# Two down projections of layer 0 as seven block products, and layer 1's late weight sums moved behind the second half of attention

## The chip, the core and the metric

The kernel runs on one core of one Trainium2 chip. A core has five engines that each work through a list of instructions of their own, in order, and wait for one another by semaphores: TensorE (PE in the profile; PEld is its loading of weights), VectorE (DVE), ScalarE (ACT), GpSimd (POOL) and SyncE (SP). Work is held in SBUF, 128 partitions wide; matmuls write to PSUM, which has eight banks of 512 float32 per partition. Transfers to and from the chip's memory (HBM) run on 16 DMA engines; here SP issues the loads of weights and POOL issues the transfers that form sums of weights.

The metric is the device time in microseconds (us), median of the runs shown. Lower is better.

## The reference, cut to what matters

A decoder trunk of two layers takes 1024 prompt tokens and 8 sample tokens, with model width 1024 and FFN width 2816 (22 slices of 128). Each layer is a mixer and a SwiGLU FFN, each with a norm before and after it and a residual sum.

```python
def swiglu(h, w_gu, w_down):
    gate, up = jnp.split(h @ w_gu, 2, axis=-1)
    return (jax.nn.silu(gate) * up) @ w_down
...
for l in range(DEPTH):
    g = g_norm[l]
    hn = rmsnorm(h, g[0])
    if l < N_A:
        mix, S = a_mixer(hn, w_in_a[l], lbs[l], hg_norm[l], mem_k[l], mem_v[l], w_o[l], hg_s0[l])
    else:
        mix = b_mixer(hn, w_in_b[l - N_A], sb_bias[l - N_A], k_all, v_all, q_pos, k_pos,
                      mem_k[l], mem_v[l], w_o[l])
    h = h + rmsnorm(mix, g[1])
    h = h + rmsnorm(swiglu(rmsnorm(h, g[2]), w_gu[l], w_down[l]), g[3])
    if l == N_A - 1:
        sb_k, sb_v = jnp.split(rmsnorm(h, g_kv) @ w_kv, 2, axis=-1)
```

`a_mixer` (layer 0) is a gated linear recurrence beside attention into a memory of 256 tokens; `b_mixer` (layer 1) is stick-breaking attention over one shared K and V beside the same kind of memory attention. Both end in a product with `w_o`, the output projection.

## The kernel before, in words

**Tokens and products.** The tokens are cut into two groups: group 0 has 512 of the prompt, group 1 has the other 512 and the 8 samples, 520 columns in all, worked as two halves of 260. Activations lie transposed, 128 features on the partitions and tokens along the columns. Every float32 operand is split into a high part in the matmul type fp32r and the remainder as a second fp32r. One product of 128x128 weights is then three matmuls for each block of columns: high by high, high by low, low by high. A weight tile of 128x512 (256 KB) is loaded by SP, cast by ACT and subtracted by DVE (`split_w`, lines 212, 217 and 218; `split_to`, lines 238 and 239, for other operands). Five raw and five split weight tiles can be under way at once.

**proj.** `proj` (line 231 issues its matmuls) makes one output block of 128 features from K input slices. Its result stands in a tile `mm` of two PSUM banks, one for each half of the columns; there are two such tiles. Beside them PSUM holds three one-bank tiles `s` and one `ns`.

**An FFN.** `ffn` works in five parts of the 22 slices, `PARTS = [(0, 5), (5, 5), (10, 4), (14, 4), (18, 4)]`. In each part it first makes the 4 or 5 gate-up slices (a `proj` for gate, one for up, `silu`, a product on line 1037, and the split of the result), then the down projection of these slices: eight `proj`, one for each 128 of the 1024 outputs, each added by DVE to the residual tile `R` in `evac_raw` (line 553, one addition of 128x520). This is the form that layer 0 uses for both groups, and layer 1 for group 0.

**Block products.** Layer 1's group 1 uses `ffn_w`. There two output blocks by two input slices are multiplied as a 2x2 block matrix with seven block products in place of eight (Strassen's scheme in Winograd's form). In `down_w` (matmul on line 841) a product is 12 matmuls of 260 columns: two output blocks, two input slices, three of the split. For each half of the outputs there are 7 products, accumulated in eight one-bank accumulators, four (`q` = 0 to 3) for each of the two output blocks (`i` = 0, 1). ACT copies an accumulator negated into another one (`minus`, line 854), and DVE adds the accumulators to `R` in pieces of 128x260 (`add`, line 850). The scheme needs four sums of weight blocks, and sums of the gate-up results of two slices.

**Sums of weights.** They are formed in DRAM by transfers that POOL issues: `weight_sums` for the gate-up weights, `down_sums` for the down weights. Each block takes eight steps (`summed`, lines 740 to 754): a one-column copy on ACT (`rr`, line 747, three buffers), a copy of that on POOL (`mk`, line 748), and then a transfer (a copy, line 753, or an accumulation, line 751) that waits for the transfers it reads from. POOL works in order, so a transfer that waits also holds up the steps behind it. What the ACT copy reads is the step's release: before, it is a column of the FFN that runs beside it.

**The order of the work.** The program is written as generators. `weave` takes the next piece of the stream that is furthest behind by its rate; a scheduler places the instructions on the engines from there. The stretch around the change, for group 1 of layer 0:

```python
f1 = ffn(1, 0, o1.x)
ws = weight_sums(1, range(5), lambda: f1.now, 4)
weave((chain(b0.sb(), b0.mem()), 24), (chain(f1.part(0), f1.part(1)), 18), (islice(ws, 16), 17))
weave((chain(f1.part(2), f1.part(3), f1.part(4)), 24), (ws, 24))
```

`b0` is the layer-1 mixer of group 0; `a0`, `a1` are layer 0's mixers of group 0 and 1; `o0.mm` and `o1.mm` are output projections, `o0.finish` and `o1.finish` the norm, the residual and the next norm behind them, `b1.sb` the attention of group 1.

Of the kernel before, what the change touches and what calls it, by code (L numbers as in the profile page):

```python
# [24 lines left out]
def tile_decoder(  # L25
# [180 lines left out]

    def split_w(W, k0, nk, m0):
        out = []
        for a in range(0, nk, 4):
# [8 lines left out]
            nc.vector.tensor_sub(ws[:, 1, :n, :], raw[:, :n, :], ws[:, 0, :n, :].bitcast(F32))  # L218
            for i in range(n):
                out.append((ws[:, 0, i, :], ws[:, 1, i, :]))  # L220
# [412 lines left out]

    def gate_up_w(l, f, ops, spl, raws, pair=None):
# [52 lines left out]
        mt = M(F32R)  # L687

        def put_sum(dst, d, a, b):
            nc.vector.tensor_sub(d, a, b)  # L690
            split_to((dst[:, 0], dst[:, 1]), d)

        if not pair:
            w = n if pair is None else h
            split_to((mt[:, 0, :w], mt[:, 1, :w]), sg[:, :w])
            if pair is not None:
                put_sum(mt[:, :, h:n], sg[:, :h], sg[:, h:n], sg[:, :h])
                pair.append((mt, sg))
            return mt
        m0, s0 = pair.pop()  # L700
        split_to((mt[:, 0, :n], mt[:, 1, :n]), sg[:, :n])
        y = [bpool.tile([P, 2, h], F32R, tag="b", name=nm("ys")) for _ in range(3)]
        put_sum(y[2], s0[:, h:n], s0[:, h:n], sg[:, h:n])
        put_sum(y[1], sg[:, h:n], sg[:, h:n], s0[:, :h])
        put_sum(y[0], sg[:, :h], sg[:, :h], sg[:, h:n])
        pair.extend((m0[:, :, :h], mt[:, :, :h], mt[:, :, h:n], y[0], m0[:, :, h:n], y[1], y[2]))
        return mt
# [26 lines left out]
    def down_sums(l, parts, after):  # L734
        for i in parts:
            t = [tc.dram_tile([P, 2, 512], F32, name=nm("dsum")) for _ in range(4)]
            dsums[i] = t
            yield from summed(t, *down_blocks(l, PARTS[i][0]), after)
# [17 lines left out]
    dsums = {}  # L756
    htok, done = [], []
# [3 lines left out]
    class ffn_w:  # L761
# [47 lines left out]
        def down_w(self, pi, f0, pairs, extra):  # L809
            l, n, h, R = self.l, NG[1], PW[1], self.R  # L810
            a11, a12, a21, a22 = down_blocks(l, f0)
            s1, s2, s3, s4 = dsums[pi]
            src = ((a11, 0), (s1, 4), (s2, 5), (a12, 1), (s3, 6), (s4, 2), (a22, 3))
            for m0 in (0, 2):
                ms = (m0, m0 + 1)
                acc = [[Q(i) for i in range(4)] for _ in ms]

                def weight(rows):
                    r = self.raws().rearrange("p k m -> p (k m)")
                    nc.sync.dma_start(r.rearrange("p (t c) -> p t c", t=2), rows[:, :, m0 * P : (m0 + 2) * P])  # L820
                    w = self.spl()
                    split_to((w[:, 0, :], w[:, 1, :]), r)
                    return w

                def slice_of(q, hf, a, first=False):
                    for i in range(2):
                        o = hf * 256 + i * P
                        for wi, (wj, xi) in enumerate(((0, 0), (0, 1), (1, 0))):
                            nc.tensor.matmul(
                                acc[i][q][:, :h], we[:, wj, o : o + P], extra[0][:, xi, a * h : (a + 1) * h],  # L830
                                start=(first and wi == 0), stop=(wi == 2), skip_group_check=True,
                            )

                def product(q, j, first=False):
                    w = weight(src[j][0])
                    for i in range(2):
                        for t in range(2):
                            x = pairs[t][src[j][1]]
                            o = t * 256 + i * P
                            for wi, (wj, xi) in enumerate(((0, 0), (0, 1), (1, 0))):  # L840
                                nc.tensor.matmul(  # L841
                                    acc[i][q][:, :h], w[:, wj, o : o + P], x[:, xi, :],
                                    start=(first and t == 0 and wi == 0), stop=(t == 1 and wi == 2),
                                    skip_group_check=True,
                                )

                def add(q, mo, a, sub=False):
                    for i, m in enumerate(ms):
                        d = R[m + mo][:, a * h : (a + 1) * h]
                        (nc.vector.tensor_sub if sub else nc.vector.tensor_add)(d, d, acc[i][q][:, :h])  # L850

                def minus(q, p):
                    for i in range(2):
                        nc.scalar.activation(acc[i][q][:, :h], acc[i][p][:, :h], AF.Copy, scale=-1.0)

                product(0, 0, True)
                minus(1, 0)
                product(3, 1, True)
                product(1, 2)
                minus(2, 1)  # L860
                product(0, 3)
# [1146 lines left out]
```

## Time and profile before

| what | value |
|---|---|
| time, median of 3 runs | 2417.74 us (2417.72 to 2418.53) |
| the profiled execution's own time | 2418.81 us |
| its span, first to last instruction | 2417.1 us |
| mean granted TensorE clock | 0.999 |
| busy PE / DVE / ACT / POOL | 99 / 66 / 51 / 6% of the span |
| matmuls | 15428 in the trace |
| moved by DMA | 369 MB |

The span's own time is 1.7 us under the time of the same execution. PE is busy for 2396.4 of 2417.1 us, so it is idle for 20.7 us in all. In a view by windows each row has the window, its length, and then the busy time of PE, PEld, DVE, ACT and POOL with the number of instructions in brackets, the granted clock, the share of the 16 DMA engines and GB/s. The parts of layer 0's second FFN that the change concerns stand at 1189 to 1258 us (part 2), 1258 to 1327 us (part 3) and 1327 to 1396 us (part 4); the last output projection `o1.mm` of layer 1 at about 1931 to 1977 us, its finish up to 2050 us, and layer 1's FFN of group 1 from there to the end.

### The profile page before, as it was taken

Reading aid. Unit: us, or ns where it says so; the run is one execution under the profiler, and the core shown is the slowest. Engines: PE = TensorE matmul, PEld = TensorE weight load, DVE = VectorE, ACT = ScalarE, POOL = GpSimd, SP = SyncE. Lnnn points to the kernel's source line nnn. Section 1 sums busy time; section 2 is a strip of 40 time slices with the busy share of each in tenths; the row PEclk is TensorE's granted clock in tenths of the full one; section 3 lists DMA queues with packets and bytes.
Section 4 is the critical chain, followed back from the end, with each engine's and each line's share of the span. In section 5 each row is a group of like instructions: output and inputs, shape, how many; then the busy total and the mean of one; then the engine's idle time right before and its main releaser. Section 6 shows DMA issues by size and latency. Waiting matters only on the chain.

```text
span 2417.1 us, 40941 instructions
## 1 busy us (share of the span) xinstructions
PE 2396.4 (99%) x15428; PEld 2134.0 (88%) x15428; DVE 1603.2 (66%) x2798; ACT 1242.9 (51%) x2482; POOL 140.1 (6%) x215
## 2 busy tenths in 40 slices
PE   8999999999999999999999999999999999999998
PEld 7888898888877888999999989877787797999998
DVE  5777566665865677555544585867687648757885
ACT  5558554544444445555433454555454445565665
POOL 3000001200000000011111100121000000000000
PEclk9999999999999999999999999999999999999999
DMA  5353255884733445456778966644453334465652
GB/s 193 105 157 106 75 157 141 198 214 135 212 111 96 137 149 183 122 136 150 183 197 213 248 181 197 194 131 122 134 180 95 94 119 127 123 192 173 181 175 75
DMA packets 499224, 369.25 MB, mean 153 GB/s; under 512 B 19757, under 2 KB 444314, under 8 KB 499026
## 3 DMA queue, kind: packets, MB, share of 16 engines
q1 hardware_dynamic: 476008, 307.87, 42.7%
q0 software_dynamic: 22912, 58.73, 10.5%
q8 instruction: 121, 1.98, 0.3%
q14 instruction: 77, 0.63, 0.1%
q10 hardware_dynamic: 106, 0.04, 0.0%
HBM read 336.74 MB, written 80.15 MB: 172 GB/s over the span
## 4 chain that ended last, share of the span: by engine, by line
PE 94%; DVE 3%; ACT 1%; issue 1%; DMA 0%; POOL 0%; DVEq 0%; ACTq 0%
PE mm L231 65%; PE q L662 7%; PE q L841 3%; PE q L620 2%; PE s L1191 1%; PE q L905 1%; PE s L1150 1%; PE s L1539 1%; PE s L1714 1%; PE mm L1104 1%; PE mm L367 1%; PE mm L1352 1%; PE q L989 1%; PE s L1753 1%; PE mm L1127 1%
## 5 line engine op out<-in xcount | busy, mean ns | idle before, releaser
L231 PE MATMUL mm<-x,ws 128*128 128x260 f32 (+1 forms) x7776 | 1327.0, 329 | 0.5 <-DVE x L239 0.3
L231 PEld LDWEIGHTS mm<-x,ws 128*128 128x128 f32 x7776 | 1148.5, 188 | 140.1 <-issue 3.4
L217 ACT CAST ws<-w 128x512 fp32r<-128x512 f32 (+1 forms) x672 | 398.1, 593 | 646.6 <-PE mm L231 566.0
L218 DVE TENSOR_TENSOR ws<-w,ws 128x512 fp32r<-128x512 f32 (+1 forms) x672 | 437.4, 654 | 216.8 <-ACT ws L217 207.1
L231 PE MATMUL mm<-m,ws 128*128 128x512 f32 (+1 forms) x2112 | 391.1, 342 | 0.0
L231 PEld LDWEIGHTS mm<-m,ws 128*128 128x128 f32 x2112 | 323.4, 188 | 45.6 <-issue 1.9
L653 DVE TENSOR_TENSOR ws<-w,ws 128x512 fp32r<-128x512 f32 x126 | 86.5, 691 | 46.7 <-ACT ws L652 44.6
L662 PE MATMUL q<-y,ws 128*128 128x260 f32 x864 | 112.9, 283 | 0.0
L662 PEld LDWEIGHTS q<-y,ws 128*128 128x128 f32 x864 | 107.6, 188 | 0.0
L553 DVE TENSOR_TENSOR r<-r,mm 128x512 f32<-128x512 f32 (+1 forms) x96 | 66.0, 687 | 60.1 <-PE mm L231 58.9
L652 ACT CAST ws<-w 128x512 fp32r<-128x512 f32 x126 | 77.8, 618 | 47.9 <-PE q L662 15.3
L271 DVE TENSOR_SCALAR t<-mm 128x512 f32<-128x512 f32 (+1 forms) x74 | 51.1, 690 | 60.3 <-PE mm L231 60.2
L275 DVE TENSOR_TENSOR t<-t,t 128x512 f32<-128x512 f32 (+1 forms) x66 | 45.7, 693 | 68.3 <-ACT t L274 68.3
L1037 DVE TENSOR_TENSOR t<-t,mm 128x512 f32<-128x512 f32 (+1 forms) x66 | 45.4, 688 | 68.7 <-PE mm L231 68.6
L662 PE MATMUL q<-x,ws 128*128 128x260 f32 x648 | 86.8, 283 | 0.0
L662 PEld LDWEIGHTS q<-x,ws 128*128 128x128 f32 x648 | 81.7, 189 | 0.0
L748 POOL COPY mk<-rr 128x1 f32<-128x1 f32 x64 | 30.1, 471 | 729.0 <-ACT rr L747 728.9
L301 DVE TENSOR_TENSOR st<-st,n 128x512 f32<-128x512 f32 (+1 forms) x91 | 62.1, 689 | 3.0 <-ACT n L300 1.8
L238 ACT CAST m<-t 128x512 fp32r<-128x512 f32 (+1 forms) x76 | 47.4, 624 | 24.5 <-DVE t L1037 17.9
L272 ACT ACTIVATE t<-t 128x512 f32<-128x512 f32 (+1 forms) x66 | 42.1, 637 | 32.5 <-DVE t L271 28.4
L1288 POOL DMA_INDIRECT c<-in_cache_sb_k,pidx x16 | 20.0, 1248 | 603.1 <-DMA out_sbv_prompt<-c 424.3
L239 DVE TENSOR_TENSOR m<-t,m 128x512 fp32r<-128x512 f32 (+1 forms) x76 | 52.5, 691 | 2.3 <-ACT m L238 1.1
(410 smaller groups left out, 2894.9 us busy)
## 6 DMA issues: line engine op xcount, KB each, us to landing
w<-in_w_gu SPq DMA_DIRECT2D x334, 256.0 KB
w<-in_w_down SPq DMA_DIRECT2D x156, 256.0 KB
w<-in_w_in_a SPq DMA_DIRECT2D x80, 256.0 KB
wsum<-in_w_gu POOLq DMA_DIRECT2D x18, 1024.0 KB
w<-wsum SPq DMA_DIRECT2D x72, 256.0 KB
w<-in_w_o SPq DMA_DIRECT2D x64, 256.0 KB
dsum<-in_w_down POOLq DMA_DIRECT2D x18, 512.0 KB
w<-in_w_mem_kv SPq DMA_DIRECT2D x32, 256.0 KB
```

What stands on the lines that cost most here:

```text
L217: nc.scalar.copy(ws[:, 0, :n, :], raw[:, :n, :])
L218: nc.vector.tensor_sub(ws[:, 1, :n, :], raw[:, :n, :], ws[:, 0, :n, :].bitcast(F32))
L231: nc.tensor.matmul(ps[:, a, : PW[g]], wt, xt[k][:, xi, o : o + PW[g]], start=(k == 0 and wi == 0), stop=(k == nk - 1 and wi == 2),)
L239: nc.vector.tensor_sub(dst[1], src, dst[0].bitcast(F32))
L271: nc.vector.tensor_scalar(sv(x, g), pv(ps, g), -44.0, None, op0=ALU.max)
L301: nc.vector.tensor_add(acc[:, :n], acc[:, :n], t[:, :n])
L553: nc.vector.tensor_add(dst, dst, pv(ps, g))
L620: nc.tensor.matmul(pp[a][:, :h], wt, xt[k][:, xi, a * h : (a + 1) * h], start=(k == 0 and wi == 0), stop=(k == ND - 1 and wi == 2),)
L652: nc.scalar.copy(w[:, 0, :], src)
L653: nc.vector.tensor_sub(w[:, 1, :], src, w[:, 0, :].bitcast(F32))
L662: nc.tensor.matmul(ps[:, :h], w[:, wj, k * P : (k + 1) * P], x[:, xi, :], start=(first and k == 0 and wi == 0), stop=(k == 3 and wi == 2), ...
L841: nc.tensor.matmul(acc[i][q][:, :h], w[:, wj, o : o + P], x[:, xi, :], start=(first and t == 0 and wi == 0), stop=(t == 1 and wi == 2), sk ...
```

## The change: what it does

Parts 2 and 3 of layer 0's FFN of group 1 (four slices each) get their down projection by block products. `down_w` and the building of the operand sums (`paired`) are taken out of `ffn_w` so that both classes call them. The code of the products is unchanged; what differs is what stands in PSUM. In `ffn_w` each accumulator is a tile of its own, one bank. In `ffn` the PSUM tiles are those of `proj`: for each output block accumulator 0 is an `s`, accumulators 1 and 2 are the two banks of one `mm` tile, and accumulator 3 is an `s` or the `ns`. The pieces run in a lagged order: the first gate-up slices of the next part come ahead of a part's down projection.

The weight sums are arranged anew. Sixteen steps for parts 2 and 3 of layer 0 (transfers of 512 KB) are added early in the program. Of the forty steps for layer 1, sixteen stay where they were, six stay beside parts 2 to 4 of the layer-0 FFN, where 24 had been, and 18 go to the last output projection (8), its finish (4) and the first parts of layer 1's last FFN (6). Their release is a column of the latest split weight (`now[0]`, written by ACT).

```diff
+    now = [None]
...
             ws = wspl.tile([P, 2, 4, P], F32R, tag="ws", name=nm("ws"))
             nc.scalar.copy(ws[:, 0, :n, :], raw[:, :n, :])
             nc.vector.tensor_sub(ws[:, 1, :n, :], raw[:, :n, :], ws[:, 0, :n, :].bitcast(F32))
+            now[0] = ws[:, 0, 0, 0:1].bitcast(F32)
...
+    def paired(sg, pair):
+        h, n = PW[1], NG[1]
+        mt = M(F32R)
...
+        if not pair:
+            w = n if pair is None else h
+            split_to((mt[:, 0, :w], mt[:, 1, :w]), sg[:, :w])
+            if pair is not None:
+                put_sum(mt[:, :, h:n], sg[:, :h], sg[:, h:n], sg[:, :h])
+                pair.append((mt, sg))
+            return mt
+        m0, s0 = pair.pop()
+        split_to((mt[:, 0, :n], mt[:, 1, :n]), sg[:, :n])
+        y = [bpool.tile([P, 2, h], F32R, tag="b", name=nm("ys")) for _ in range(3)]
+        put_sum(y[2], s0[:, h:n], s0[:, h:n], sg[:, h:n])
+        put_sum(y[1], sg[:, h:n], sg[:, h:n], s0[:, :h])
+        put_sum(y[0], sg[:, :h], sg[:, :h], sg[:, h:n])
...
+    def down_w(l, pi, R, pairs, extra, raws, spl, banks, each):
...
+        for m0 in (0, 2):
+            ms = (m0, m0 + 1)
+            acc = [banks(i) for i in range(2)]
...
+            product(0, 0, True)
+            minus(1, 0)
+            product(3, 1, True)
+            product(1, 2)
+            minus(2, 1)
+            product(0, 3)
...
+            add(3, 4, 1)
+            add(0, 0, 0)
+            yield
+            product(1, 4)
+            add(3, 0, 1, True)
+            add(1, 4, 1)
+            product(2, 5)
...
+            add(2, 0, 1)
+            product(1, 6)
...
+            add(1, 4, 0)
+            each(ms)
+            yield
...
     class ffn:
-        def __init__(self, g, l, xt, rows=False):
+        def __init__(self, g, l, xt, blocks=()):
...
         def down(self, pi):
...
+            if pi in self.blocks:
+
+                def four(i):
+                    two = mmp.tile([P, 2, 512], F32, tag="mm", name=nm("mm"))
+                    return [S(), two[:, 0, :], two[:, 1, :], NS() if i else S()]
...
+                yield from down_w(l, pi, self.R, pairs, mids[4:], self.raws, self.spl, four, each)
+                return
...
-    weave((a0.mem(), 8), (a1.fq(), 8))
+    ds = down_sums(0, (2, 3), lambda: now[0])
+    weave((a0.mem(), 8), (a1.fq(), 8), (islice(ds, 7), 8))
     o0 = out_proj(0, 0, M)
-    drain(o0.mm(a0.xo))
-    weave((o0.finish(), 17), (chain(a1.v(), a1.qm(A)), 8))
+    weave((o0.mm(a0.xo), 8), (islice(ds, 5), 5))
+    weave((o0.finish(), 17), (chain(a1.v(), a1.qm(A)), 8), (ds, 4))
...
-    f1 = ffn(1, 0, o1.x)
-    ws = weight_sums(1, range(5), lambda: f1.now, 4)
+    f1 = ffn(1, 0, o1.x, (2, 3))
+    here = lambda: now[0]
+    ws = weight_sums(1, range(5), here, 4)
...
-    weave((chain(f1.part(2), f1.part(3), f1.part(4)), 24), (ws, 24))
+    lagged = chain(
+        f1.gate_up(2), f1.gate_up(3, 0, 1), f1.down(2), f1.gate_up(3, 1), f1.gate_up(4, 0, 1), f1.down(3),
+        f1.gate_up(4, 1), f1.down(4),
+    )
+    weave((lagged, 24), (islice(ws, 6), 6))
...
-    drain(o1.mm(b1.xo))
-    weave((o1.finish(), 17), (f0.part(4), 8))
+    weave((o1.mm(b1.xo), 8), (islice(ws, 8), 8))
+    weave((o1.finish(), 17), (f0.part(4), 8), (islice(ws, 4), 4))
...
-    weave((chain(f0.finish(False), store_y(0, f0.R), token_rows(1, o1.R)), 17), (chain(f1.part(0), f1.part(1)), 7))
+    weave(
+        (chain(f0.finish(False), store_y(0, f0.R), token_rows(1, o1.R)), 17), (chain(f1.part(0), f1.part(1)), 7),
+        (ws, 8),
+    )
```

**PE, the down projection of part 2.** A row is one group of matmuls with the tile they write, the tiles they read, their shape, their count and the engine whose semaphore the first of them waits for; `m` are gate-up results, `ys` sums of them, `ws` split weights. Before, one output block of 128 features is one `mm` tile and 24 matmuls, and it stands so eight times:

```order
L231 MATMUL mm_12508<-m_12058,ws_12505 128x260 [waits PE_49]
L231 MATMUL mm_12508<-m_12058,ws_12505 128x260 x5
L231 MATMUL mm_12508<-m_12196,ws_12505 128x260 x6
L231 MATMUL mm_12508<-m_12330,ws_12505 128x260 x6
L231 MATMUL mm_12508<-m_12464,ws_12505 128x260 x6
```

Now, in the second half of that down projection, on PE, `product(1, 4)` ends and `product(2, 5)` (operand `m`) and `product(1, 6)` (operand `ys`, last) follow, and then the first matmul of the next gate-up slice:

```order
L796 MATMUL mm_12851<-ys_12565,ws_12934 128x260 x3
...
L796 MATMUL mm_12854<-ys_12565,ws_12934 128x260 x3
L796 MATMUL mm_12851<-m_12287,ws_12955 128x260 [waits DVE_49]
L796 MATMUL mm_12851<-m_12287,ws_12955 128x260 x2
L796 MATMUL mm_12851<-m_12560,ws_12955 128x260 x3
L796 MATMUL mm_12854<-m_12287,ws_12955 128x260 [waits DVE_49]
...
L796 MATMUL mm_12851<-ys_12290,ws_12974 128x260 [waits DVE_49]
...
L796 MATMUL mm_12854<-ys_12290,ws_12974 128x260 [waits DVE_49]
...
L234 MATMUL mm_13006<-x_9309,ws_12998 128x260 [waits DVE_49]
```

The tiles `mm_12851` and `mm_12854` are the pairs of accumulators 1 and 2 of the two output blocks. `product(2, 5)` waits for DVE here. In `ffn_w`, whose PE rows for the same three products read as follows, the accumulators are tiles `q`, and `product(2, 5)` waits for nothing:

```order
L841 MATMUL q_22457<-ys_22309,ws_22551 128x260 x3
...
L841 MATMUL q_22461<-ys_22309,ws_22551 128x260 x3
L841 MATMUL q_22458<-m_22017,ws_22572 128x260 x3
L841 MATMUL q_22458<-m_22304,ws_22572 128x260 x3
L841 MATMUL q_22462<-m_22017,ws_22572 128x260 x3
L841 MATMUL q_22462<-m_22304,ws_22572 128x260 x3
...
L841 MATMUL q_22457<-ys_22020,ws_22597 128x260 [waits DVE_49]
```

What moved: an accumulator that had a tile to itself shares one with its neighbour, and matmuls into either bank come behind DVE's reading of the other.

**DVE, the end of the same half.** The additions are the rows of line 805; the rows of lines 242 and 220 are splits of weights:

```order
L805 TENSOR_TENSOR r_10260<-r_10260,s_12852 128x260 [waits PE_49]
L220 TENSOR_TENSOR ws_13064<-w_13062,ws_13064 128x512 [waits DMAHW3_49,DVE_49,Activation_49]
L805 TENSOR_TENSOR r_10260<-r_10260,s_12855 128x260 [waits PE_49]
L220 TENSOR_TENSOR ws_13069<-w_13067,ws_13069 128x512 [waits DMAHW4_49,DVE_49,Activation_49]
L805 TENSOR_TENSOR r_10260<-r_10260,mm_12851 128x260 [waits DVE_49,PE_49]
L805 TENSOR_TENSOR r_10260<-r_10260,mm_12854 128x260 [waits DVE_49,PE_49]
L805 TENSOR_TENSOR r_10260<-r_10260,mm_12851 128x260 [waits PE_49]
L805 TENSOR_TENSOR r_10260<-r_10260,mm_12854 128x260 [waits DVE_49,PE_49]
L220 TENSOR_TENSOR ws_13139<-w_13137,ws_13139 128x512 [waits DMAHW5_49,Activation_49]
L805 TENSOR_TENSOR r_10260<-r_10260,mm_12851 128x260 [waits PE_49]
L805 TENSOR_TENSOR r_10260<-r_10260,mm_12854 128x260 [waits DVE_49,PE_49]
```

Before, DVE's row for a whole output block was one addition of 128x520; now an accumulator is added in pieces of 128x260, with splits of the coming weights between them.

**POOL, the late sums.** Before, the last sums of layer 1 (`wsum`) are issued ahead of the gathers of the cache (`c`, for the attention of group 1):

```order
L753 DMA wsum_13680<-wsum_13678 512x512 [waits DMASW5_49]
L748 COPY mk_14376<-rr_14374 128x1 [waits Activation_49,Pool_49]
L751 DMA wsum_13680<-in_w_gu 512x512 [waits DMASW7_49,DMASW6_49]
L1288 DMA c_16467<-in_cache_sb_k,pidx 128x512 [waits DVE_49]
L1288 DMA c_16467<-in_cache_sb_k,pidx 128x512
```

Now 18 of them, in POOL's row behind the last of those gathers, start so, each transfer behind its own mark:

```order
L1340 DMA c_17688<-in_cache_sb_v,pidx 128x512 [waits DMASW4_49,DMASW5_49,DVE_49,PE_49]
L1340 DMA c_17688<-in_cache_sb_v,pidx 128x512
L755 COPY mk_19570<-rr_19568 128x1 [waits Activation_49,Pool_49]
L760 DMA wsum_12155<-wsum_12153 512x512 [waits DMASW6_49]
L755 COPY mk_19638<-rr_19636 128x1 [waits Activation_49,Pool_49]
L758 DMA wsum_12155<-in_w_gu 512x512 [waits DMASW7_49,DMASW6_49]
L755 COPY mk_19710<-rr_19708 128x1 [waits Activation_49,Pool_49]
L760 DMA wsum_19706<-in_w_gu 512x512 [waits DMASW0_49]
```

What moved: the transfers of three blocks of sums less six steps have gone from beside the FFN of layer 0 to beside the last output projection and what follows it.

197 lines of the change are left out of this document (97 added, 100 removed).

## The prediction

> **What bounds the kernel now.** I read the page's busy line and its chain first, to learn which engine sets the end:
>
> ```profile
> PE 2396.4 (99%) x15428; PEld 2134.0 (88%) x15428; DVE 1603.2 (66%) x2798; ACT 1242.9 (51%) x2482; POOL 140.1 (6%) x215
> PE 94%; DVE 3%; ACT 1%; issue 1%; DMA 0%; POOL 0%; DVEq 0%; ACTq 0%
> ```
>
> TensorE does. It is busy for all but 20.7 of 2417.1 us, and 94% of the chain that ended last is its own work. So a matmul taken out is worth its own duration wherever PE waits for nothing, and anything given to another engine is free until PE waits for it. Next comes the chain cut to the stages of the change, to see whether PE waits there (start, length, what):
>
> ```profile
> 1189.71 209.82 PE mm L231 x1730
> ...
> 2268.89 20.12 PE q L841 x168
> ...
> 2329.41 20.15 PE q L841 x168
> ```
>
> The first row is the whole of parts 2 to 4 of the layer-0 FFN: 209.82 us of matmuls without one wait between them. The others are the two down projections of layer 1 that already run as block products: 168 matmuls each, also without a wait. Then the windows of these stages and of those to which sums are moved:
>
> ```profile
> 217.00:277.00 60.00, 59.88 (x452) 57.54 (x451) 41.70 (x88) 40.31 (x98) 0.00 (x0) 1.00 0.22 63
> 277.00:323.00 46.00, 46.00 (x204) 37.52 (x204) 16.79 (x26) 20.16 (x37) 0.00 (x0) 1.00 0.38 115
> 323.00:380.00 57.00, 56.92 (x452) 54.85 (x451) 41.34 (x68) 29.79 (x55) 0.00 (x0) 1.00 0.47 143
> ...
> 1189.00:1235.00 46.00, 46.00 (x385) 45.92 (x384) 22.41 (x33) 20.98 (x37) 6.59 (x9) 1.00 0.61 166
> 1235.00:1258.00 23.00, 23.00 (x194) 23.00 (x193) 11.11 (x17) 5.64 (x12) 3.80 (x7) 1.00 0.95 219
> 1304.00:1327.00 23.00, 23.00 (x194) 23.00 (x193) 11.09 (x17) 5.74 (x12) 3.80 (x7) 1.00 0.95 225
> 1373.00:1396.00 23.00, 23.00 (x185) 22.61 (x185) 15.54 (x24) 10.31 (x20) 4.46 (x7) 1.00 1.05 272
> 1931.00:1981.00 50.00, 49.98 (x395) 48.50 (x395) 16.46 (x26) 20.08 (x36) 0.00 (x0) 1.00 0.40 122
> 1981.00:2025.00 44.00, 44.00 (x192) 35.16 (x190) 34.60 (x55) 25.26 (x43) 0.00 (x0) 1.00 0.43 127
> 2025.00:2060.00 35.00, 33.25 (x187) 28.47 (x187) 31.90 (x51) 20.31 (x34) 0.00 (x0) 1.00 0.35 104
> 2268.90:2289.00 20.10, 20.10 (x170) 20.10 (x170) 18.53 (x42) 11.89 (x24) 0.00 (x0) 1.00 0.67 193
> ```
>
> In all but one of them PE is busy from edge to edge at a granted clock of 1.00. Only 2025 to 2060 has 1.75 us of idle PE, and DVE is busy for 31.90 of 35 there. In the last row, block products, DVE is at 18.53 of 20.10.
>
> **The change part by part: the matmuls removed.** The direct step's pitch comes from its eight additions:
>
> ```profile
> L553 DVE TENSOR_TENSOR r<-r,mm x8: 695/696/697, 1236.0 to 1256.1; 128x520 f32<-128x520 f32 x8
> ```
>
> Seven intervals in 20.1 us are 2.87 us for each output block of 24 matmuls, 119.7 ns each; eight blocks are 22.98 us. The block products' 168 matmuls took 20.12 and 20.15 us, 119.8 ns each. So 24 matmuls fewer are 2.87 us less in each part, and two parts are 5.75 us. The Trainium skill ("TensorE: Matmul & The Clock Gate", section "Wait — 56ns, not 53.3ns?") has warm matmuls start N / 2.4 GHz + 2.5 ns apart; an estimate by that page is 110.8 ns for 260 columns, and 5.32 us for the 48. This trace has 119.7 ns, and the row decides.
>
> **The wait that it adds.** Accumulators 1 and 2 now share one `mm` tile, and `product(2, 5)` waits for DVE's `add(1, 4, 1)`, which reads the other bank of that tile; likewise `product(1, 6)` for `add(2, 0, 1)`, and the next gate-up slice for `add(1, 4, 0)`. The nearest rows are the second half of layer 1's step, where the same additions and products stand without that wait:
>
> ```profile
> 2283.99 0.43 DVE L850 TENSOR_TENSOR r<-r,q 128x260 f32<-128x260 f32 x1 [0.20 <-PE q L841]
> ...
> 2284.52 1.62 PE L841 MATMUL q<-ys,ws 128*128 128x260 f32 x12
> ...
> 2285.42 0.69 DVE L653 TENSOR_TENSOR ws<-w,ws 128x512 fp32r<-128x512 f32 x1
> 2285.97 1.61 PE L841 MATMUL q<-m,ws 128*128 128x260 f32 x12
> 2286.03 0.75 DVE L850 TENSOR_TENSOR r<-r,q 128x260 f32<-128x260 f32 x2
> 2286.87 0.69 DVE L653 TENSOR_TENSOR ws<-w,ws 128x512 fp32r<-128x512 f32 x1
> 2287.42 1.59 PE L841 MATMUL q<-ys,ws 128*128 128x260 f32 x12
> 2287.48 0.75 DVE L850 TENSOR_TENSOR r<-r,q 128x260 f32<-128x260 f32 x2
> ...
> 2047.06 0.61 DVE r L553
> 2047.67 0.14 issue
> 2047.81 2.04 PE q L620 x15
> ```
>
> DVE starts 0.20 us after the matmul it waited for, an addition takes 0.43, and PE goes on 0.14 us after DVE (the last three rows, of the chain): 0.77 us from a last matmul to the first that waits for its addition. The six matmuls of the other output block cover 0.72 of that, so the wait costs 0.05 us if DVE is free. It is not always: at 2285.42 a split of a weight stands ahead of the addition, which starts at 2286.03, ends at 2286.46, and would let PE go at 2286.60 in place of 2285.97, a stall of 0.63.
>
> I worked through the four halves with the DVE order of the changed program. First halves: matmuls of the next half stand between, and no split comes just ahead of the addition; 0 in part 2, 0.1 in part 3. Second half of part 2: a split stands just ahead, as in the rows, 0.63; then 0.05; then a split ahead of the last addition holds the next gate-up slice for about 0.35. Second half of part 3: 0.05, then about 0.3 behind a split, then 0.05. The sum is 1.5 us. The ends: 0 if DVE runs earlier than I worked out, and 7.6 us if all twelve such waits cost 0.63. I take 1.5, by the order of the splits.
>
> **Other work in parts 2 and 3.** DVE's 8 additions of 0.70 become 24 of 0.38 (pairs take 0.75), its splits 8 to 14 of 0.69: 9.0 and 9.7 us in 20.1, against 11.11 of 23.00 before. That is the load of the 18.53 in 20.10 which layer 1's PE bore without a wait; its cover is thin, and the stalls above are what it costs. ACT gets 8 negations per part, as in layer 1, where it is at 11.89 of 20.10: nothing. The operand sums (four subtractions and four splits of 128x260 for each pair of slices, by the same 0.43 some 3.4 us of DVE per 23 us) lie beside gate-up, where DVE is at 22.41 of 46.00: nothing. SP's twelve more weight loads of 256 KB, 3.1 MB, go where sums leave: nothing.
>
> **The sums taken away and the early ones.** Taking 18 steps from the FFN gains nothing, since PE stood at 23.00 of 23.00 with them. The 16 new steps, 8.4 MB, land at 217 to 380 us, where the DMA share is 0.22 to 0.47. By the page's two queues,
>
> ```profile
> q1 hardware_dynamic: 476008, 307.87, 42.7%
> q0 software_dynamic: 22912, 58.73, 10.5%
> ```
>
> a MB takes 42.7% of 2417.1 us / 307.87 = 3.35 us of all 16 engines for loads, and 4.3 us in the sums' queue. That makes 28 to 36 us in 163: nothing. Their one-column ACT copies read what ACT itself wrote, so ACT waits for no other engine's result.
>
> **The late sums.** Beside `o1.mm` the pace is one step of 1.05 MB every 5.74 us for 46 us. That adds 8.4 MB, 28 to 36 us by the same two figures, to the 0.40 there: a share of 1.0 to 1.2. The nearest rows are the old down steps. There, too, a weight was used every 2.87 us and a step was released every 5.74 us:
>
> ```profile
> 1240.55 0.66 POOL L753 DMA_DIRECT2D wsum<-wsum  x1 [0.31 <-issue]
> 1245.70 0.32 POOL L748 COPY mk<-rr 128x1 f32<-128x1 f32 x1 [4.50 <-ACT rr L747]
> 1248.97 1.02 POOL L751 DMA_DIRECT2D wsum<-in_w_gu  x1 [2.94 <-DMA wsum<-wsum]
> ...
> 1260.40 0.66 POOL L753 DMA_DIRECT2D wsum<-wsum  x1 [8.63 <-DMA wsum<-in_w_gu]
> 1261.05 0.20 POOL L748 COPY mk<-rr 128x1 f32<-128x1 f32 x1
> ```
>
> POOL waited 2.94 and 8.63 us for transfers, which throttles the steps; the share stood at 0.95 to 1.05; and PE never waited for a weight. What is queued behind POOL's wait is the next mark, and ACT only stops once three `rr` copies are unread, 17 us of lag at this pace; the largest here is about 4. I take 0 for `o1.mm`; its ends are 0 and (1.18 - 1) x 46 = 8.3 us. In the finish four steps are 14 to 18 us of transfer in 79 us at 0.35 to 0.43. DVE, which bounds its end, gets nothing; ACT gets four copies. I take 0.
>
> **The sum.** 5.75 less 1.5 is 4.25 us. The profiled execution's 2418.81 becomes 2414.56. It lies 1.07 us above the median of the runs, 2417.74, so the median becomes 2413.5, 0.18% less. A change of under 0.2%, 4.8 us, cannot be told from none in this kernel; the bounds are 2412.9 and 2422.6.
>
> **Rivals.** *The waits cost nothing.* DVE's additions come a little earlier than in layer 1, since PE's first stall lets it catch up, and the shared tiles cost at most 0.05 at each place. For it: DVE still has 1.57 us of idle in the 20.10. Against: the split at 2285.42. Then 5.75 less 0.3 gives 2412.3. The Trainium skill ("PSUM — Partial Sum Buffer", section "PSUM bank collisions raise a hardware error") says that two engines may use different banks at the same time and asks to guard by bank and quadrant. By that page the chip needs no wait between accumulators 1 and 2, and the estimate would be the whole gain; the order of the program has the wait all the same, and no run yet shows what it costs.
>
> *DVE becomes the bound of the new steps.* Each stall delays the additions' releases, a split is then late for the next product, and waits of 0.63 appear in all four halves. It has eaten the gain once the twelve waits average 0.48 us. For it: 18.53 of 20.10. Against: each PE stall gives DVE the same time. Three quarters of them would cost 5.7 us, no change, 2417.7; all cost 7.6, 2419.6.
>
> *The late sums make weights late*, the case on the other side. At `o1.mm` the demand is over what the 16 engines carry, weights share the engines with the sums, and PE waits once a weight lands later than the five raw tiles' lead, 14.4 us. All of the excess, 8.3 us, with the gain of 4.25 gives 2421.8; with the residual's loads delayed as well, it passes 2422.6. Against: three windows at 0.95 to 1.05 without a wait, and POOL's own waits, which slow the sums first.
>
> That the change doesn't save its matmuls is excluded by the order: PE has 48 fewer.
>
> **How the numbers follow.** My forecast (2412.9 to 2416) gets 0.47, waits for nothing (2411.5 to 2412.9) 0.30, DVE as the bound (2416 to 2420) 0.13, late weights (2418 to 2425) 0.10. Faster by over 0.2% is the second, 0.30; slower by over 0.2% is most of the last, 0.09; the rest, 0.61, lies within. The range from 2411.5 to 2419.5 leaves out most of late weights and the tails. The forecast's own range is 2412.9 to 2416.
>
> **What would show it.** The chain of the changed kernel has two rows or groups of 168 matmuls on the block products' line with a stretch of 20.6 to 21.2 us each, and PE's waits list DVE's additions there with about 1.5 us. The direct steps' 2.87 us pitch remains in part 4. PE stays at 46 of 46 in `o1.mm` with a DMA share near 1. I am wrong if PE's waits there name a weight's DMA or split, if the stalls pass 5 us, or if PE waits in the early stages.

## The result

| | median | range | runs |
|---|---|---|---|
| before | 2418.48 us | 2417.72 to 2419.71 | 22 |
| changed | 2414.72 us | 2413.88 to 2418.12 | 22 |

The changed kernel takes 0.9985 of the time before, 95% interval 0.9979 to 0.9991: 3.76 us less, where 4.25 us less was forecast. The gain is real and small; the forecast range, 2411.5 to 2419.5, holds it. The median forecast was 2413.5 us; of the 1.2 us that it was off, 0.74 are the median before, 2417.74 in 3 runs and 2418.48 in 22. Two lines of the changed kernel's page (the busy line, and the engines of the chain that ended last):

```profile
PE 2391.0 (99%) x15380; PEld 2127.9 (88%) x15380; DVE 1626.2 (67%) x2874; ACT 1264.9 (52%) x2542; POOL 169.3 (7%) x247
PE 94%; DVE 3%; ACT 1%; issue 1%; DMA 1%; DVEq 0%; SPq 0%; ACTq 0%
```

PE has 48 matmuls fewer and is still the bound. DVE, ACT and POOL each took on 22 to 29 us of work.

What the two down projections took (the two steps, from here on; those of the sums are called sum steps) is read best from one DVE instruction that both kernels have: the first step of `silu`, which follows each gate product. Two of them are 11.48 us apart inside a gate-up stage, so an interval that also contains a down projection gives its length. Before (start, length, engine, line, tiles; parts 2 and 3, the last slice before the down projection and the first behind it):

```profile
1215.82 0.70 DVE L271 TENSOR_SCALAR t<-mm 128x520 f32<-128x520 f32 x1 [1.53 <-PE mm L231]
1227.30 0.70 DVE L271 TENSOR_SCALAR t<-mm 128x520 f32<-128x520 f32 x1 [1.53 <-PE mm L231]
1261.84 0.70 DVE L271 TENSOR_SCALAR t<-mm 128x520 f32<-128x520 f32 x1 [1.49 <-PE mm L231]
...
1296.28 0.70 DVE L271 TENSOR_SCALAR t<-mm 128x520 f32<-128x520 f32 x1 [1.53 <-PE mm L231]
1330.81 0.70 DVE L271 TENSOR_SCALAR t<-mm 128x520 f32<-128x520 f32 x1 [1.49 <-PE mm L231]
```

After, the same view:

```profile
1237.93 0.70 DVE L274 TENSOR_SCALAR t<-mm 128x520 f32<-128x520 f32 x1 [0.85 <-PE mm L234]
1270.81 0.70 DVE L274 TENSOR_SCALAR t<-mm 128x520 f32<-128x520 f32 x1 [1.53 <-PE mm L234]
...
1305.25 0.70 DVE L274 TENSOR_SCALAR t<-mm 128x520 f32<-128x520 f32 x1 [0.84 <-PE mm L234]
1337.73 0.70 DVE L274 TENSOR_SCALAR t<-mm 128x520 f32<-128x520 f32 x1 [1.53 <-PE mm L234]
```

Before, 34.54 and 34.53 less 11.48 are 23.06 and 23.05 us. After, 32.88 and 32.48 less 11.48 are 21.40 and 21.00 us. Together 3.71 us are gone, which is the whole result within its interval. Twice 168 matmuls without a wait would be 20.12 each, so 1.28 and 0.88 us were given back inside the steps.

The PE timeline of the changed kernel shows where, at the end of each step (start, length, count; in brackets the idle time and what ended it):

```profile
1259.27 1.61 PE L796 MATMUL mm<-ys,ws 128*128 128x260 f32 x12
1261.25 1.69 PE L796 MATMUL mm<-m,ws 128*128 128x260 f32 x12 [0.37 <-DVE r L805]
1262.78 1.67 PE L796 MATMUL mm<-ys,ws 128*128 128x260 f32 x12
1264.76 1.47 PE L234 MATMUL mm<-x,ws 128*128 128x260 f32 x10 [0.31 <-DVE r L805]
...
1326.76 1.60 PE L796 MATMUL mm<-ys,ws 128*128 128x260 f32 x12
1328.20 1.66 PE L796 MATMUL mm<-m,ws 128*128 128x260 f32 x12
1330.18 1.70 PE L796 MATMUL mm<-ys,ws 128*128 128x260 f32 x12 [0.32 <-DVE r L805]
1331.72 1.55 PE L234 MATMUL mm<-x,ws 128*128 128x260 f32 x11
```

Twelve matmuls start 1.44 us after the twelve before them when nothing waits. From 1259.27 to 1261.25 are 1.98 us: a stall of 0.54 at `product(2, 5)`, 0.54 at the exit to the next gate-up slice (1262.78 to 1264.76), and in part 3 0.54 at `product(1, 6)` (1328.20 to 1330.18). The bracket shows less, 0.31 to 0.37, because a group's recorded time is longer than its pitch (1.60 us for twelve matmuls that start 1.44 us after the twelve before them), so start-to-start is the measure. With pieces of 0.06 to 0.10 elsewhere the steps come to 1.17 and 0.81 us, by their first and last matmuls.

DVE's timeline tells what held the additions up:

```profile
1260.17 0.69 DVE L220 TENSOR_TENSOR ws<-w,ws 128x512 fp32r<-128x512 f32 x1
1260.78 0.75 DVE L805 TENSOR_TENSOR r<-r,mm 128x260 f32<-128x260 f32 x2
1262.27 0.43 DVE L805 TENSOR_TENSOR r<-r,mm 128x260 f32<-128x260 f32 x1 [0.73 <-PE mm L796]
1262.98 0.42 DVE L805 TENSOR_TENSOR r<-r,mm 128x260 f32<-128x260 f32 x1 [0.28 <-PE mm L796]
1263.67 0.69 DVE L220 TENSOR_TENSOR ws<-w,ws 128x512 fp32r<-128x512 f32 x1 [0.27 <-ACT ws L219]
1264.28 0.75 DVE L805 TENSOR_TENSOR r<-r,mm 128x260 f32<-128x260 f32 x2
```

A weight's split stands directly ahead of the addition both times, as it had been read from the order; the second one itself waited 0.27 us for ACT's cast.

The stages that took the sums, in windows of the changed kernel (PE, PEld, DVE, ACT, POOL, clock, DMA share, GB/s):

```profile
217.00:277.00 60.00, 59.88 (x451) 57.47 (x450) 41.72 (x89) 41.38 (x104) 8.87 (x14) 1.00 0.51 120
...
323.00:380.00 57.00, 56.92 (x449) 54.72 (x449) 41.31 (x69) 29.79 (x57) 3.84 (x6) 1.00 0.61 168
...
1921.00:1979.00 58.00, 58.00 (x439) 55.14 (x438) 20.77 (x34) 25.51 (x52) 9.27 (x15) 1.00 0.93 242
...
2025.00:2056.00 31.00, 29.23 (x172) 25.31 (x171) 30.95 (x50) 18.58 (x33) 4.54 (x6) 1.00 0.75 178
```

The early stages keep the very busy times of PE that they had. The last output projection runs at a DMA share of 0.93 where it had 0.40, and PE is busy for 58.00 of 58.00. The idle 1.77 us in the last row is the 1.75 us of before.

### The profile page after: what moved, and what is told of

Read it like the earlier page. It is cut to its first block, busy times and chain, and to the rows that moved or that the text cites. A ratio compares the mean times of both kernels' runs of the same rounds, so it can differ in the third digit from the quotient of the medians.

```text
span 2412.8 us, 41092 instructions
## 1 busy us (share of the span) xinstructions
PE 2391.0 (99%) x15380; PEld 2127.9 (88%) x15380; DVE 1626.2 (67%) x2874; ACT 1264.9 (52%) x2542; POOL 169.3 (7%) x247
## 3 DMA queue, kind: packets, MB, share of 16 engines
q8 instruction: 121, 1.98, 0.3%
## 4 chain that ended last, share of the span: by engine, by line
PE 94%; DVE 3%; ACT 1%; issue 1%; DMA 1%; DVEq 0%; SPq 0%; ACTq 0%
PE mm L234 63%; PE q L689 7%; PE q L796 3%; PE q L623 2%; PE s L1243 1%; PE q L916 1%; PE s L1202 1%; PE s L1766 1%; PE s L1591 1%; PE mm L1156 1%; PE s L1805 1%; PE mm L370 1%; PE mm L1404 1%; PE q L1000 1%; PE mm L1179 1%
## 5 line engine op out<-in xcount | busy, mean ns | idle before, releaser
L219 ACT CAST ws<-w 128x512 fp32r<-128x512 f32 (+1 forms) x656 | 388.0, 592 | 599.6 <-PE mm L234 515.6
L220 DVE TENSOR_TENSOR ws<-w,ws 128x512 fp32r<-128x512 f32 (+1 forms) x656 | 426.3, 653 | 209.5 <-ACT ws L219 205.5
L234 PE MATMUL mm<-m,ws 128*128 128x512 f32 (+1 forms) x1728 | 344.4, 355 | 0.0
L234 PEld LDWEIGHTS mm<-m,ws 128*128 128x128 f32 x1728 | 277.1, 188 | 45.6 <-issue 2.1
L755 POOL COPY mk<-rr 128x1 f32<-128x1 f32 x80 | 45.2, 565 | 1526.9 <-ACT rr L754 1526.9
L680 DVE TENSOR_TENSOR ws<-w,ws 128x512 fp32r<-128x512 f32 x126 | 86.5, 691 | 46.4 <-ACT ws L679 44.2
L679 ACT CAST ws<-w 128x512 fp32r<-128x512 f32 x126 | 77.8, 618 | 47.5 <-PE q L689 15.3
L556 DVE TENSOR_TENSOR r<-r,mm 128x512 f32<-128x512 f32 (+1 forms) x80 | 54.9, 686 | 37.9 <-PE mm L234 36.5
L278 DVE TENSOR_TENSOR t<-t,t 128x512 f32<-128x512 f32 (+1 forms) x58 | 40.1, 692 | 57.2 <-ACT t L277 57.2
L1068 DVE TENSOR_TENSOR t<-t,mm 128x512 f32<-128x512 f32 (+1 forms) x58 | 39.9, 687 | 56.7 <-PE mm L234 56.5
L241 ACT CAST ws<-w 128x512 fp32r<-128x512 f32 x72 | 44.4, 618 | 37.5 <-PE mm L234 10.7
L242 DVE TENSOR_TENSOR ws<-w,ws 128x512 fp32r<-128x512 f32 x72 | 49.0, 688 | 11.6 <-ACT ws L241 10.6
```

The costliest lines, as they stand in the source:

```text
L219: nc.scalar.copy(ws[:, 0, :n, :], raw[:, :n, :])
L234: nc.tensor.matmul(ps[:, a, : PW[g]], wt, xt[k][:, xi, o : o + PW[g]], start=(k == 0 and wi == 0), stop=(k == nk - 1 and wi == 2),)
L241: nc.scalar.copy(dst[0], src)
L242: nc.vector.tensor_sub(dst[1], src, dst[0].bitcast(F32))
L556: nc.vector.tensor_add(dst, dst, pv(ps, g))
L679: nc.scalar.copy(w[:, 0, :], src)
```

## The experiments

Each stands against the kernel before on the same chip; three chips were used, and its median there was 2418.84 to 2419.25 us. The changed kernel itself was run once more on the chip whose median was 2418.84, and is the yardstick there; on the other two it is taken as 3.7 us under the kernel before.

> The changed kernel once more, on the chip of the runs beside it: 3.3 to 4.3 us less than the kernel before, and two block steps of 21.2 to 21.5 and 20.9 to 21.1 us in the trace.

2415.15 us against 2418.84, 0.9986 (0.9977 to 0.9995); the two steps took 21.39 and 20.99 us. As expected.

**The sums moved, the down projections left direct.**

```diff
-    f1 = ffn(1, 0, o1.x, (2, 3))
+    f1 = ffn(1, 0, o1.x)
...
-    weave((lagged, 24), (islice(ws, 6), 6))
+    weave((chain(f1.part(2), f1.part(3), f1.part(4)), 24), (islice(ws, 6), 6))
```

> All down projections of layer 0 direct and in the old order, all sums where the change puts them (the sixteen early ones are formed and not used). Theory (the moved sums cost and gain nothing): the time of the kernel before within 0.5 us, PE without a wait in the last output projection. Rival (late sums make weights late): up to 8.3 us slower than before, with PE waits for weights in the last output projection. Rival (the sums left the FFN with a gain): faster than before by 0.5 us or more.

2419.16 us against 2419.11, 1.0001 (0.9992 to 1.0010). Moving the sums, and forming sixteen more, neither costs nor gains anything that can be measured. All of the result comes from the two down projections.

**The accumulators dealt out to the tiles differently.** The code of the products stays; one `mm` tile holds accumulator 2 of both output blocks and the other accumulator 1 of both. Then no matmul shares a tile with the accumulator that DVE has just begun to read.

```diff
+                two = []
+
                 def four(i):
-                    two = mmp.tile([P, 2, 512], F32, tag="mm", name=nm("mm"))
-                    return [S(), two[:, 0, :], two[:, 1, :], NS() if i else S()]
+                    if not i:
+                        two[:] = [mmp.tile([P, 2, 512], F32, tag="mm", name=nm("mm")) for _ in range(2)]
+                    return [S(), two[1][:, i, :], two[0][:, i, :], NS() if i else S()]
```

> The two mm tiles of a half are dealt out by accumulator instead of by output block: one tile holds accumulator 2 of both blocks, the other accumulator 1 of both, and the tile of accumulator 2 is the older one, which the next gate-up slice takes. Theory (the 2.0 us that the two steps take beyond 168 matmuls are the waits on the shared tile, 0.54 us at product(2, 5) and product(1, 6) and at the exit): product(2, 5) no longer waits for DVE, product(1, 6) has a whole product as cover, the exit finds its tile free; at most 0.6 us of stall is left, so 1.4 to 2.0 us less than the changed kernel, 2412.7 to 2413.3 us. Rival (DVE's load is the bound, the tile is only where it shows): the stall moves to the weights' splits, less than 0.5 us changes.

2414.06 us against 2419.11, 0.9978 (0.9969 to 0.9987): 5.05 us less, some 1.3 more than the change gains, and longer than the 2412.7 to 2413.3 us expected. Its PE timeline at the end of part 2's step, the two `silu` rows around that step, and the DVE row of the addition for which `product(2, 5)` waited in the change:

```profile
1259.96 1.71 PE L796 MATMUL mm<-ys,ws 128*128 128x260 f32 x12
1261.51 1.60 PE L796 MATMUL mm<-m,ws 128*128 128x260 f32 x12
1262.94 1.60 PE L796 MATMUL mm<-ys,ws 128*128 128x260 f32 x12
1264.38 3.88 PE L234 MATMUL mm<-x,ws 128*128 128x260 f32 x31
```

```profile
1238.54 0.70 DVE L274 TENSOR_SCALAR t<-mm 128x520 f32<-128x520 f32 x1 [0.85 <-PE mm L234]
1270.34 0.70 DVE L274 TENSOR_SCALAR t<-mm 128x520 f32<-128x520 f32 x1 [1.53 <-PE mm L234]
```

```profile
1261.70 0.76 DVE L805 TENSOR_TENSOR r<-r,mm 128x260 f32<-128x260 f32 x2 [0.20 <-PE mm L796]
```

The products follow one another at 1.43 to 1.55 us, and PE waits for nothing between 1150 and 1400 us. The step is 31.80 less 11.48, 20.32 us, part 3's is 20.26; the stalls are down from 2.16 to 0.34 us by the same count. DVE has as many splits of weights and additions between 1240 and 1340 us as before the edit (44 and 48), in part in another order, and its additions came no earlier: the one at 1261.70 had not begun when `product(2, 5)` started at 1261.51. So the wait on the shared tile is the cause; that the splits ahead of the additions set its size is read from the rows of the change. Run once more beside the changed kernel:

> Tiles dealt out by accumulator once more, beside the changed kernel on one chip. Theory (only the waits on the shared tile go): 1.5 to 2.0 us less than the changed kernel, 5.0 to 5.9 us less than the kernel before. Rival (no gain beyond what can be measured): within 0.5 us of the changed kernel.

2415.07 us against 2418.84, 0.9983 (0.9974 to 0.9992), and so beside the changed kernel's 2415.15 no gain in the median, as the rival had it. The steps in the trace are again 20.32 and 20.26 us. What took it back in many of its executions is told in the last section; over the whole time the intervals of the two forms overlap. The stage shows the 1.8 us, and so do the executions whose mean granted clock was 0.999: their medians are 2413.14 us (5 of 11) and 2415.11 us (9 of 11), 1.97 us apart.

The same with the two tiles' turns exchanged, to test the exit:

```diff
-                    return [S(), two[1][:, i, :], two[0][:, i, :], NS() if i else S()]
+                    return [S(), two[0][:, i, :], two[1][:, i, :], NS() if i else S()]
```

> As the run by accumulator, but with the tile of accumulator 1 the older one. Theory: the next gate-up slice takes the tile whose last two additions end last, 0.20 + 0.75 + 0.14 = 1.1 us after the last matmul, and a split may stand ahead; 1.1 to 1.6 us at each of the two exits, so 2.2 to 3.2 us more than the run by accumulator, 0.5 to 1.5 us more than the changed kernel, with PE waits on line 234 for DVE's additions. Rival (DVE's load is the bound): the same time as the run by accumulator within 0.5 us.

2413.53 us against 2419.11, 0.9979 (0.9970 to 0.9988), steps of 20.35 and 20.27 us, no wait of PE: the time of the run by accumulator, as the rival had it, but not for its reason: nothing waits for DVE. The theory of the exit falls in this point. The next gate-up slice is not held to the older tile; its first matmul started before the last additions of accumulator 1, so it had the tile that was free:

```profile
1263.43 1.60 PE L796 MATMUL mm<-ys,ws 128*128 128x260 f32 x12
1264.86 3.41 PE L234 MATMUL mm<-x,ws 128*128 128x260 f32 x27
```

```profile
1265.07 0.76 DVE L805 TENSOR_TENSOR r<-r,mm 128x260 f32<-128x260 f32 x2
```

In the change both tiles hold an accumulator 1, which is read last, so neither is free at the exit.

**The block steps with the late sums left where they were.**

```diff
-    weave((lagged, 24), (islice(ws, 6), 6))
+    weave((lagged, 24), (ws, 24))
...
-    weave((o1.mm(b1.xo), 8), (islice(ws, 8), 8))
-    weave((o1.finish(), 17), (f0.part(4), 8), (islice(ws, 4), 4))
+    drain(o1.mm(b1.xo))
+    weave((o1.finish(), 17), (f0.part(4), 8))
...
-        (ws, 8),
```

> The two block steps as in the change, but the 24 late sums stay beside parts 2 to 4 of the FFN. Theory (the sums hold themselves up through POOL, weights keep their turn): demand there is about 12.3 us of weights and 18 us of sums in 20 us, a share of 1.5, the sums only get later; 0 to 1 us more than the changed kernel. Rival (the DMA engines are the bound where both meet): weights land late in the block steps, which use one in 1.44 us, and the kernel is 3 to 10 us slower than the changed one, with PE, ACT or DVE waiting for the loads of w.

2417.65 us against 2419.11, 0.9992 (0.9983 to 1.0001): 1.46 us less than before, where the change has 3.7 less. The two intervals overlap, so the loss of some 2 us is not clear in the time alone; the trace shows where it comes from. Between the two theories, nearer to the rival: a load of a down weight came late. ACT's list of waits and DVE's and PE's timelines of this run:

```profile
ACT ws L241 <- DMA w<-in_w_down: 5.8, 1, 5.8
```

```profile
1224.74 0.69 DVE L220 TENSOR_TENSOR ws<-w,ws 128x512 fp32r<-128x512 f32 x1 [0.46 <-ACT ws L219]
1231.12 0.69 DVE L242 TENSOR_TENSOR ws<-w,ws 128x512 fp32r<-128x512 f32 x1 [5.68 <-ACT ws L241]
1231.73 0.69 DVE L274 TENSOR_SCALAR t<-mm 128x520 f32<-128x520 f32 x1
```

```profile
1252.88 0.99 PE L796 MATMUL mm<-m,ws 128*128 128x260 f32 x6 [1.20 <-DVE r L805]
```

While ACT stood for the load, DVE stood for ACT, and its `silu` step came 16.25 us after the last one in place of 11.48. DVE had not caught up 20 us later, when PE waited 1.20 us for an addition. From the first `silu` row of part 2 to the second of part 4 the stage took 147.37 us, 1.65 more than in the changed kernel (145.72). The execution traced is the shortest of its eleven, 2415.83 us.

Whether the shared tile is what handed DVE's lateness on, the same with the tiles by accumulator had to tell (the two edits above together):

> Tiles dealt out by accumulator, and the 24 late sums left beside parts 2 to 4. Where the sums stayed with the tiles of the change, the two steps lost about 1.7 us in the stage to a load of w that came 5.8 us late: DVE's splits queued up and PE stood 1.2 us at a shared tile. Theory (the shared tile is what hands DVE's lateness on to PE): with the tiles by accumulator less than 0.6 us of that is left, 2413.5 to 2415 us by this chip's time of the changed kernel less 1 us. Rival (the late weight costs by itself): the loss of 1.5 to 2.5 us against the run by accumulator with the sums moved stays.

2415.03 us against 2418.84, 0.9983 (0.9974 to 0.9992). The time alone would fit the theory, but the trace does not: the stage took 145.35 us against 143.90 in the run by accumulator, so 1.45 of the 1.65 us stay. ACT waited 5.9 us for a load of a down weight here too, and PE met it at ACT's negation, the second row; the first lies behind this stage, in part 4's down projection, after a load of `w_o` for which ACT had waited 6.4 us:

```profile
PE mm L234 <- DVE r L556: 1.9, 1, 1.9
PE mm L796 <- ACT mm L809: 0.5, 1, 0.5
```

The late weights cost by themselves; the execution traced, 2416.98 us, is one of the longer of its eleven. The median is no worse than that of the run by accumulator on the same chip, but that run had the lower clock of the last section in 6 of 11 executions and this one in 1: among executions with a mean granted clock of 0.999 the medians are 2414.84 us (10 of 11) and 2413.14 us (5 of 11), 1.70 us more with the sums left.

**Twice as many sums beside the last output projection.**

```diff
-    weave((o1.mm(b1.xo), 8), (islice(ws, 8), 8))
-    weave((o1.finish(), 17), (f0.part(4), 8), (islice(ws, 4), 4))
+    weave((o1.mm(b1.xo), 8), (islice(ws, 16), 16))
+    weave((o1.finish(), 17), (f0.part(4), 8), (islice(ws, 2), 4))
```

> The changed kernel with 16 late sum steps beside the last output projection in place of 8 (a step every 2.87 us), 2 in its finish and none later. Theory (POOL's in-order waits slow the sums, and the three one-column buffers stop ACT once POOL is three steps behind): a step takes about 5 us there when the DMA engines are full, so POOL falls behind by some 2.5 us a step, ACT stops after the seventh or so, weights are split late; 5 to 25 us slower than the changed kernel, with ACT waiting for POOL at the one-column copies. Rival (late weights: the DMA share itself is what matters): a similar loss, but ACT waits for the loads of w and not for POOL. Rival (the sums only run later): the time of the changed kernel within 1 us.

2432.72 us against 2418.84, 1.0060 (1.0044 to 1.0075), some 17.6 us more than the changed kernel. ACT's timeline has the waits that the theory named, and PE's list of waits follows:

```profile
1954.02 0.19 ACT L754 COPY rr<-ws 128x1 f32<-128x1 f32 x1 [6.50 <-POOL mk L755]
...
1962.99 0.19 ACT L754 COPY rr<-ws 128x1 f32<-128x1 f32 x1 [6.72 <-POOL mk L755]
1968.91 0.19 ACT L754 COPY rr<-ws 128x1 f32<-128x1 f32 x1 [5.73 <-POOL mk L755]
```

```profile
PE mm L234 <- ACT a L554: 8.7, 1, 8.7
PE mm L234 <- DVE t L1068: 4.5, 1, 4.5
```

PE was idle for 14.2 us between 1920 and 2030 us, and its granted clock from 1921 to 1979 us was 0.91. In the same run ACT also waited 14.9 us for loads of `w`, so this run alone does not settle which one did it. The next one takes ACT out of the sums: from the second late step on, POOL's mark reads a constant.

```diff
-            tok = small([P, 1], tag="rr")
-            nc.scalar.copy(tok, after())
+            tok = epsb
+            if not free[0]:
+                tok = small([P, 1], tag="rr")
+                nc.scalar.copy(tok, after())
...
+    next(ws)
+    free[0] = True
+    weave((o1.mm(b1.xo), 8), (islice(ws, 15), 16))
```

> Again 16 late sum steps beside the last output projection and 2 in its finish, but from the second on POOL's mark reads a constant and no longer a copy that ACT makes: POOL runs through the sums as fast as its own waits let it, and ACT has no instruction that waits for POOL. Theory (ACT was stopped by POOL: with the ACT copies it stood three times for 6.50, 6.72 and 5.73 us at one, and only then PE ran dry): nearly all of the 14 us goes, 0 to 3 us more than the changed kernel. Rival (the loads of w come late because the DMA engines are full): 8 us or more of the loss stays, with ACT waiting for loads of w.

2435.79 us against 2419.25, 1.0069 (1.0052 to 1.0086). Nothing came back, as the rival had it. But it does not clear the copies in the run before: without them the loads landed later still, so this run shows that late loads alone cost this much, and which of the two cost it there stays open. (Freed from ACT, POOL also issued its first sum steps some 20 us ahead of the projection.) ACT waits for loads now, by its list, and the view of the DMA issues says how late they land (size, median us from issue to landing; window 1921 to 1979 us):

```profile
ACT ws L220 <- DMA w<-in_w_o: 24.7, 5, 5.3
```

```profile
w<-in_w_o SPq DMA_DIRECT2D x7, 256.0 KB, 27.6
w<-in_w_gu SPq DMA_DIRECT2D x7, 256.0 KB, 18.1
```

The changed kernel in the same window:

```profile
w<-in_w_gu SPq DMA_DIRECT2D x11, 256.0 KB, 7.7
...
w<-in_w_o SPq DMA_DIRECT2D x8, 256.0 KB, 4.6
```

A weight is used every 2.87 us and five raw tiles can be under way, a lead of 14.4 us. Loads of 4.6 to 7.7 us fit into it, those of 18.1 and 27.6 us do not; with the dense sums and their ACT copies the medians were 14.7 and 12.6 us, at the edge. In the changed kernel ACT waits for no load between 1900 and 2070 us. So at twice the pace weights come late, and POOL's own waits do not slow the sums enough to protect them.

## Why the prediction was right, point by point

- **The matmuls removed: 5.75 us.** Right within 0.12 us. Without the added wait the two steps took 20.32 and 20.26 us against 23.06 and 23.05, 5.53 us less; with the last 0.34 us of stalls that makes 5.87.
- **The wait that it adds: 1.5 us.** The mechanism is right, shown by dealing the accumulators out differently. The term was too small: 2.0 us by the PE rows, 2.16 by the `silu` rows. Part 2's `product(2, 5)` was put at 0.63 and measured 0.54; its exit at 0.35 and measured 0.54, since the split ahead of the addition waited for ACT's cast as well; part 3's `product(1, 6)` at 0.3 and measured 0.54. By the `silu` rows 5.87 less 2.16 is the 3.71 measured: the wait was 0.66 larger than forecast and the matmuls' share 0.12 larger, which together make the difference to 4.25. So the first step, 21.29 us from its first matmul to the first behind it, lies just over the 20.6 to 21.2 forecast for it, and the second, 20.93, within. PE's list of waits for DVE's additions has 1.0 us and not 1.5 there, as its brackets show less than start-to-start.
- **The rival that the waits cost nothing** is excluded by the same rows: DVE did not run earlier. The Trainium skill ("PSUM — Partial Sum Buffer", section "PSUM bank collisions raise a hardware error"), cited there, by which two engines may use different banks at the same time, is not at odds with it: with the two accumulators in different tiles the stall went. The wait was the program's, for a whole tile.
- **DVE as the bound of the new steps** did not come about; stalls of more than 0.1 us stand in three of the twelve places, and they go with DVE doing as much as before.
- **Other work and the early sums: nothing.** Right: the windows of the early stages are the same, and the run with the sums alone gave 1.0001.
- **The sums taken away: "gains nothing".** True for direct down projections, as that run shows; not for the block steps, which use a weight in half the time. Left there, the same sums cost 1.65 us in the traced stage and, with the tiles by accumulator, 1.70 in the time at a clock of 0.999. The move is part of what makes the gain.
- **The late sums: 0.** The number is right, its reason half so, and so in part luck. I argued that POOL's waits throttle the sums before the weights suffer. At twice the pace they do not: weights landed after 27.6 us, and the kernel was some 18 to 20 us slower than the changed one. What protects the change is that one sum step in 5.74 us leaves the loads inside their lead. The rival's point from which it decides, a load later than 14.4 us, fits the runs: medians of 4.6 and 7.7 us cost nothing, of 18.1 and 27.6 us they did.
- **"A change of under 0.2% cannot be told from none."** With 22 runs of each it could: 0.15%, and the interval leaves out no change.

## What to carry to other kernels

An accumulator that shares a tile with another one inherits its waits: before packing two into one tile, look which of them is read while the other is written, and pair those that are used at the same time. A transfer that is moved to a stage with a slack engine has to be judged there by the landing time of the loads beside it against their lead, not by whether the share has reached one: here loads of 4.6 to 7.7 us were free and those of 18.1 to 27.6 us cost some 20, while the share from 1921 to 1979 us was 0.93 in the changed kernel and 0.95 with the sums at twice the pace, which lost 17.6 us. And a step made shorter raises the demand for its operands: what could run beside the old step for nothing may not beside the new one.

## What the runs showed of the hardware that was not expected

The same program, the one by accumulator, had two lengths behind a short idle time of PE. In both of its traces, from two chips, PE is idle for 1.77 us at about 2040 us, at the end of `o1.finish`. In one, the granted clock then falls:

```profile
2038.00:2042.00 4.00, 2.23 (x11) 1.56 (x10) 4.00 (x7) 2.94 (x7) 3.50 (x4) 1.00 0.52 95
2042.00:2046.00 4.00, 4.00 (x19) 2.97 (x19) 3.95 (x7) 0.94 (x2) 0.01 (x1) 0.63 1.13 208
```

In the other, whose row from 2038 to 2042 us has the same busy times and 1.00, it stays:

```profile
2042.00:2046.00 4.00, 4.00 (x30) 3.52 (x29) 4.00 (x8) 2.22 (x5) 0.00 (x0) 1.00 1.12 206
```

From 2042 to 2046 us PE got through 19 matmuls at a granted clock of 0.63, and 30 at 1.00. The stretch from there to the next stage was 48.67 us long in the one and 47.05 in the other, 1.62 us apart. A mean clock of 0.998 in place of 0.999 was seen in 14 of 32 executions of the kernels by accumulator and in 4 of 33 of the changed kernel, which has the same idle time some 1.7 us later in the program; those executions took 0.9 to 2.7 us more than the others of their kernel, by medians. That is why the 1.8 us gained in the stage do not show in the medians over all executions. With the tiles by accumulator and the sums left beside the FFN, where the idle time comes some 4.4 us later, it was 1 of 11. The Trainium skill ("TensorE: Matmul & The Clock Gate", section "What's actually happening") ties the throttle to an idle window of about 3.4 us. Here the clock fell behind a recorded idle time of 1.77 us in one trace and not in the other; that it fell in the same place in the executions without a trace is not shown, and why it did so oftener where the idle time comes earlier was not tried.
